# One core of a hybrid retention and attention layer: row-times-weight sums on VectorE alone, early splits on ScalarE and VectorE, and the gate's columns loaded behind the first pair's keys and values

## The chip, the core and the metric

The kernel runs on one core of one Trainium2 chip. The metric is the device time of one execution in microseconds (us), the median of the runs shown. A profiled execution has a time of its own, which is given beside its span.

## What is computed

The reference is one layer over 2048 latent tokens and 256 context tokens of width 1024, in float32. Cut to what matters here:

```python
shift, scale, gate = jnp.split(jax.nn.silu(c) @ w_ada[l] + b_ada[l], 3, axis=-1)
shift_c, scale_c, gate_c = jnp.split(jax.nn.silu(c_ctx) @ w_ada[l] + b_ada[l], 3, axis=-1)
h = rms_norm(x) * (1.0 + scale[:, None, :]) + shift[:, None, :]
hc = rms_norm(ctx) * (1.0 + scale_c) + shift_c
rq, rk, rv, rg, aq, ak, av, ag = project(h, w_in[l])
crq, crk, crv, crg, caq, cak, cav, cag = project(hc, w_in[l])
...
s_fwd = retention_final_state(crk, crv, log_gamma[0], reverse=False)
ret_x, _, _ = retention_branch(rq, rk, rv, rg, log_gamma, ret_gn_w[l], s_fwd, s_bwd)
att_x = merge_heads(windowed_gqa(aq, ak, av, cak, cav, att_sink[l])) * jax.nn.silu(ag)
mixed = jnp.concatenate([ret_x, att_x], axis=-1) @ w_out[l]
x = x + gate[:, None, :] * mixed
return rms_norm(x) * final_norm_w
```

The modulation needs three vectors of width 1024 for the latent tokens (shift, scale, gate) and two for the context (shift_c, scale_c). Each is a product of a row, silu(c) or silu(c_ctx), with a 1024 x 1024 part of w_ada.

## The kernel before, in words

**Two phases.** Up to about 600 us the kernel projects the tokens, group by group of 512 (groups 3 and 2 first, then the context, then 1 and 0), and stores queries, keys, values, gates and the states of the retention in HBM. From there on it goes block by block through retention, attention and the output projection. The change lies in the first phase.

**Precision.** A float32 product is made of three passes on TensorE: each operand is split into a high half, rounded to the engine's fast float32 form (`rounded`, line 105), and a low half, the difference. A unit of projection is 256 columns of w_in for one group: `load_w` (line 314) loads them in two parts of 512 KB each, rounds the high half and subtracts for the low half, in four pieces of 128x512 each. TensorE then makes 2 x 24 matmuls (8 blocks of the width, 3 passes each). So TensorE waits for the low halves as much as for the high ones. `split` (line 374) does the same to results that are stored as halves: the attention's queries and keys.

**The modulation sums.** `weigh` (line 209) multiplies a 128x1024 tile of the transposed w_ada with the row and sums along the row, which gives 128 numbers of a vector. With `idle` false it is one VectorE instruction with an accumulator (line 215); with `idle` true a product on GpSimd (POOL, line 212) and a copy with an accumulator on ScalarE (ACT, line 213). `ada` (line 220) calls it for the shift and the scale (j = 0 and 1) of one block of the width; for the context the scale (j = 1) is done with `idle`. `gate_columns` (line 604) calls it for eight blocks of the gate, every other one with `idle`. The context's steps (`prep_ctx`, line 246) are: load the context and make its statistics, then for each block `column(k)` (line 260): two `weigh`, the scaling on ACT (line 268), the high half on POOL (`rounded`, line 269) and the low half on VectorE (line 270).

**What sets the order.** The steps of the context and of the gate's columns stand in a list, `spare`, and `background(n)` (line 404) issues the next n of them behind a unit. The units run in the order of the list `order` (line 1040): aq1, rq0, rq1, then the first pair's keys and values rk0 and rv0 (context, group 3, group 2), then rk1 and rv1, and so on. `weights` (line 1045) loads the next units' weights ahead: two slots hold split weights (pool wp) and seven slots of 512 KB hold what has just been loaded (pool ld: parts of w_in, tiles of w_ada, rows of x). A load waits, on the one load queue of SyncE (SP), until a slot is free, and what stands behind it on that queue waits too. The framework arranges the instructions of each engine by a schedule of its own; each engine then runs its queue in that order.

**The context's keys and values** (`ctx_rk`, `ctx_rv`) are the first units that need the modulated context: tiles crk and crv on TensorE, from hc (the context's halves) and the weights w_brk and w_brv. Behind them come rk for group 3 (tile rk, 2 x 24 matmuls), the retention's context state (tile cu), and so on.

**Names in the rows.** wss is a tile of w_ada for shift and scale, wgt one for the gate; room holds the context and the two rows; w_baq, w_brq, w_brk, w_brv are split weights, wr_ in front of a name means as loaded; hi_aq and lo_aq are the halves of the attention's queries, m_aq and m_rq the products of the rotary step; xr_x are rows of x for the statistics of the next group.

Of the kernel before, what the change touches and what calls it, by code (L numbers as in the profile page):

```python
# [11 lines left out]
AF = mybir.ActivationFunctionType  # L12
# [27 lines left out]
def tile_hymba(  # L40
# [168 lines left out]
    def weigh(w, row, a, idle=False):  # L209

        if idle:
            pool.tensor_tensor(w, w, row, op=ALU.mult)
            act.activation(w, w, AF.Copy, accum_out=a)
        else:
            dve.scalar_tensor_tensor(w, w, 1.0, row, op0=ALU.mult, op1=ALU.mult, accum_out=a)
# [4 lines left out]
    def ada(pl, tag, row, kc, which, after=(None, None)):  # L220
        for j in range(2):
            w = pl.tile([P, D], F32, tag=tag, name=f"wss{which}_{kc}_{j}")
            nc.sync.dma_start(w, wss[kc][:, j, :])
            with behind(after[j]):
                weigh(w, row, acc2[:, kc, which, j : j + 1], which and j)
        dve.tensor_tensor(mod[:, kc, which], acc2[:, kc, which], nbada[:, kc:16:8], op=ALU.add)
# [24 lines left out]
    def prep_ctx():  # L251
# [9 lines left out]
        def column(k):  # L261
            if k == 0:
                r = st.spread()
                for x in xk:
                    dve.tensor_tensor(x, x, r, op=ALU.mult)
            ada(ld, "ld", row1, k, 1)
            x = xk[k]
            act.activation(x, x, AF.Identity, bias=mod[:, k, 1, 0:1], scale=mod[:, k, 1, 1:2])
            rounded(hc[0][:, k, :], x)
            dve.tensor_tensor(hc[1][:, k, :], x, hc[0][:, k, :], op=ALU.subtract)  # L270
# [43 lines left out]
    def load_w(name, uid, parts=(0, 1), w=None, lo="dve", fine=None, hi="pool"):  # L314
# [3 lines left out]
        for i in parts:  # L318
# [3 lines left out]
            for j in range(2):  # L322
# [6 lines left out]
                (pool if lo == "pool" or (lo == "mix" and j) else dve).tensor_tensor(w[:, 1, ks, :], r2, w[:, 0, ks, :], op=ALU.subtract)  # L329
# [44 lines left out]
    def split(src, name, n=GT, np_=P):  # L374
        hi = tmp(f"hi_{name}", dt=F32R)[:np_, :n]
        lo = tmp(f"lo_{name}", dt=F32R)[:np_, :n]
        rounded(hi, src)
# [27 lines left out]
    spare = []  # L405
# [200 lines left out]
    def gate_columns():  # L606
# [3 lines left out]
        def column(k):  # L610
            wg = ld.tile([P, D], F32, tag="ld", name=f"wgt{k}")
            nc.sync.dma_start(wg, wgt[k])
            weigh(wg, row2, gcol[:, k : k + 1], k % 2)
# [422 lines left out]
    spare += gate_columns()  # L1036
# [8 lines left out]
    def weights(i, ahead=1):  # L1045

        for x in order[i : i + 1 + ahead]:
            if x not in W:
                early = x in order[:3]
                W[x] = load_w(x[0], x[1] + x[0], lo="mix" if early else "dve", hi="act" if early else "pool")  # L1050
        return W[order[i]]

    def retention(i, gs, before=lambda name, g: None):

        w = weights(i), weights(i + 1, 0)
        for n, g in enumerate(gs):
            for j in range(2):
                before(order[i + j][0], g)
                unit(order[i + j][0], g, w[j])
                background()  # L1060
# [18 lines left out]
    X = []  # L1079
    retention(5, groups, ahead)  # L1080
# [325 lines left out]
```

## Time and profile before

| what | value |
| --- | --- |
| median of 3 runs | 1181.79 us (1178.88 to 1182.34) |
| profiled execution, its own time | 1177.99 us |
| its span, first to last instruction | 1175.4 us |
| TensorE (PE) busy | 1133.2 us, 96% |
| VectorE (DVE) busy | 798.2 us, 68% |
| ScalarE (ACT) busy | 465.7 us, 40% |
| GpSimd (POOL) busy | 404.5 us, 34% |

The page gives busy times over the whole span, which mix two phases with different limits. TensorE is the engine that has the least idle time, so the question in each stretch is whether it has work, at which clock, and for what it waits where it has none. The views by stretch, of waits, of the chain of work and of the engines' instructions in order of time are those that the rows below come from.

### The profile page before, as it was taken

The page shows a single profiled execution, that of the slowest core. Times are in us where ns is not written, and L with a number is a line of the kernel's source. Part 1 is how long each engine was busy: PE and PEld are TensorE (multiplying, and loading weights), DVE is VectorE, ACT ScalarE, POOL GpSimd, SP SyncE. Part 2 cuts the span into 40 slices and gives each one's busy share as a digit, 9 for nine tenths or more (in the row PEclk, how much of TensorE's full clock was granted, in tenths as well). Part 3 has the DMA queues.
Part 4 walks back from the last instruction along what each step waited for, and adds up shares of the span by engine and source line. Part 5 has one row for each costly group of instructions (what it writes and reads, how often), then busy time and mean ns, then how long its engine had stood idle before and what let it go on. Part 6 is the DMA issues. An engine that isn't in the chain of part 4 may idle for free.

```text
span 1175.4 us, 18111 instructions
## 1 busy us (share of the span) xinstructions
PE 1133.2 (96%) x6290; PEld 973.1 (83%) x6290; DVE 798.2 (68%) x1883; ACT 465.7 (40%) x1025; POOL 404.5 (34%) x517
## 2 busy tenths in 40 slices
PE   7999978999999999999999988999999999999997
PEld 3887857999988889998888877888888888888885
DVE  6974876544783645657666447777777777777774
ACT  3344423432342002331001336555555555555562
POOL 1102654100221200002224335555555555555542
PEclk9998989999999999999999999999999999999999
DMA  8948678542564542533356385444444444444310
GB/s 305 324 152 259 235 228 308 177 132 86 176 215 157 162 125 77 175 119 117 97 162 201 83 210 187 131 130 131 130 130 131 131 130 131 130 130 131 95 37 36
DMA packets 139537, 182.24 MB, mean 155 GB/s; under 512 B 11315, under 2 KB 103091, under 8 KB 139318
## 3 DMA queue, kind: packets, MB, share of 16 engines
q1 hardware_dynamic: 126630, 174.54, 47.3%
q10 hardware_dynamic: 12816, 6.56, 1.8%
q8 instruction: 49, 0.80, 0.3%
q14 instruction: 42, 0.34, 0.1%
HBM read 130.19 MB, written 50.86 MB: 154 GB/s over the span
## 4 chain that ended last, share of the span: by engine, by line
PE 69%; DVE 19%; POOL 3%; ACT 3%; DMA 3%; issue 2%; SPq 1%; DVEq 0%; POOLq 0%; ACTq 0%
PE pz L1205 10%; PE rv L354 8%; PE rk L341 7%; PE aq L341 6%; PE ag L341 6%; PE o L1168 4%; PE rg L341 4%; PE rq L341 4%; PE pt L1155 3%; DVE p L749 3%; DVE phl L1158 3%; PE S L743 3%; PE u L470 2%; PE ak L341 2%; PE S L747 2%
## 5 line engine op out<-in xcount | busy, mean ns | idle before, releaser
L1157 ACT ACTIVATE phl<-pt 128x512 fp32r<-128x512 f32 x156 | 92.7, 595 | 98.8 <-PE pt L1155 96.0
L765 POOL TENSOR_SCALAR p<-p,m 128x640 f32<-128x640 f32 (+1 forms) x128 | 104.1, 814 | 69.9 <-DVE m L764 68.5
L1158 DVE TENSOR_TENSOR phl<-pt,phl 128x512 fp32r<-128x512 f32 x156 | 106.8, 686 | 29.9 <-ACT phl L1157 29.2
L756 ACT ACTIVATE p<-p,m 128x641 f32<-128x641 f32 (+1 forms) x128 | 104.5, 816 | 47.3 <-DVE m L753 47.0
L749 DVE CUSTOM_DVE_ANT_0 p<-S,msk 128x640 f32<-128x640 f32 (+1 forms) x128 | 102.5, 801 | 23.4 <-PE S L747 22.0
L1205 PE MATMUL pz<-wg1h,ma 128*128 128x512 f32 x256 | 106.0, 419 | 0.1
L1205 PE MATMUL pz<-wg0h,mr 128*128 128x512 f32 x256 | 104.0, 409 | 0.6 <-POOL mr L1194 0.4
L1155 PE MATMUL pt<-ident,p 128*128 128x128 f32 x624 | 94.0, 273 | 0.0
L743 PE MATMUL S<-kwin,aq 128*128 128x384 f32 (+1 forms) x256 | 79.2, 332 | 4.2 <-DVE m L749 2.8
L1155 PEld LDWEIGHTS pt<-ident,p 128*128 128x128 f32 x624 | 75.8, 141 | 8.7 <-issue 0.4
L446 ACT ACTIVATE vw<-v,wdec 128x128 fp32r<-128x128 f32 x128 | 43.5, 393 | 80.1 <-DVE v L459 80.1
L747 PE MATMUL S<-kctx,aq 128*128 128x256 f32 x256 | 71.1, 280 | 0.0
L1168 PE MATMUL o<-phl,vwin 128*128 128x512 f32 x184 | 63.1, 422 | 0.8 <-DVE phl L1158 0.6
L743 PEld LDWEIGHTS S<-kwin,aq 128*128 128x128 f32 x256 | 48.0, 188 | 10.7 <-DVE m L749 3.4
L1205 PEld LDWEIGHTS pz<-wg0h,mr 128*128 128x128 f32 x256 | 48.1, 188 | 9.3 <-POOL mr L1194 0.8
L1205 PEld LDWEIGHTS pz<-wg1h,ma 128*128 128x128 f32 x256 | 48.1, 188 | 7.9 <-POOL ma L1183 0.5
L747 PEld LDWEIGHTS S<-kctx,aq 128*128 128x128 f32 x256 | 48.2, 188 | 5.3
L1168 PE MATMUL o<-phl,vctx 128*128 128x512 f32 x128 | 44.7, 414 | 6.8 <-DVE phl L1158 6.7
L1205 PE MATMUL pz<-wg0l,mr 128*128 128x512 f32 x128 | 50.5, 395 | 0.0
L1205 PE MATMUL pz<-wg1l,ma 128*128 128x512 f32 x128 | 50.3, 393 | 0.0
L448 DVE SCALAR_TENSOR_TENSOR vw<-v,wdec,vw 128x128 fp32r<-128x128 f32 x128 | 39.9, 358 | 6.2 <-ACT vw L446 6.2
L780 POOL TENSOR_TENSOR qd<-qkv,decq 128x512 f32<-128x512 f32 x30 | 42.3, 1428 | 1.1
(430 smaller groups left out, 3067.7 us busy)
## 6 DMA issues: line engine op xcount, KB each, us to landing
wss<-in_wss SPq DMA_DIRECT2D x32, 512.0 KB, 6.3
qkv<-d_qkv SPq DMA_DIRECT2D x15, 768.0 KB, 6.2
aq<-d_aq SPq DMA_DIRECT2D x64, 128.0 KB, 3.9
xb<-in_xn SPq DMA_DIRECT2D x16, 512.0 KB, 4.2
out<-xb SPq DMA_DIRECT2D x31, 256.0 KB, 2.3
st<-d_st SPq DMA_DIRECT2D x15, 512.0 KB, 3.8
x<-in_xt SPq DMA_DIRECT2D x12, 512.0 KB, 5.3
xr_x<-in_xn SPq DMA_DIRECT2D x12, 512.0 KB, 3.8
```

The lines of the kernel that those rows point to most:

```text
L341: pe.matmul(ps, w[:, a, k, c0 : c0 + P], ht[b][:, k, :], start=(k == 0 and i == 0), stop=(k == NK - 1 and i == 2),)
L354: pe.matmul(ps, ht[a][:, k, t * P : (t + 1) * P], w[:, b, k, :], start=(k == 0 and i == 0), stop=(k == NK - 1 and i == 2),)
L743: i = pe.matmul(psc[:, o:512].rearrange("p (s t) -> p s t", t=P), AQ[b][:, h, :], C2["kwin"][:, kv, hl, ksel], start=(hl == 0), stop=(hl = ...
L747: pe.matmul(psc[:, 512:768], AQ[b][:, h, :], C2["kctx"][:, kv, hl], start=(hl == 0), stop=(hl == 1))
L749: dve.tensor_tensor_reduce(out=pb[:, j, 0:n], in0=psc[:, o : o + n], in1=mk, op0=ALU.add, op1=ALU.max, scale=1.0, scalar=-3e38, accum_out= ...
L756: act.activation(pb[:, j, 0 : n + 1], pb[:, j, 0 : n + 1], AF.Exp, bias=m4[:, 1, j : j + 1], scale=0.125, accum_out=m4[:, 2, j : j + 1],)
L765: pool.tensor_scalar(pb[:, j, 0:n], pb[:, j, 0:n], m4[:, 2, j : j + 1], 0.0, op0=ALU.mult, op1=ALU.add)
L1155: pe.transpose(ppt[:, j], pb[:, j, kt * P : (kt + 1) * P], ident)
L1157: PE["phl"] = act.activation(phl[:, 0], ppt, AF.Copy)
L1158: dve.tensor_tensor(phl[:, 1], ppt, phl[:, 0], op=ALU.subtract)
L1168: pe.matmul(PO[kv], vt, PH[kt][:, hl], start=(kt == 0 and hl == 0), stop=(kt == nkt - 1 and hl == 1))
L1205: pe.matmul(PZ[n2], m[:, a, k % RH, :], WG[k // 4][c][:, k % 4, s], start=(k == 0 and i == 0), stop=(k == NK - 1 and i == 2),)
```

## The change

Four edits. `weigh` has no `idle` form any more, so that all of its calls are one VectorE instruction. The high halves in `split` and of the context are rounded on ACT and not on POOL. For the first three units' weights (aq1, rq0, rq1) the second half of the low parts, which POOL made, is made on VectorE. The gate's columns are put into `spare` only before the second pair's keys and values (rk1 and rv1), and `background` takes two steps at a time there.

```diff
-    def weigh(w, row, a, idle=False):
-
-        if idle:
-            pool.tensor_tensor(w, w, row, op=ALU.mult)
-            act.activation(w, w, AF.Copy, accum_out=a)
-        else:
-            dve.scalar_tensor_tensor(w, w, 1.0, row, op0=ALU.mult, op1=ALU.mult, accum_out=a)
+    def weigh(w, row, a):
+
+        dve.scalar_tensor_tensor(w, w, 1.0, row, op0=ALU.mult, op1=ALU.mult, accum_out=a)
...
-                weigh(w, row, acc2[:, kc, which, j : j + 1], which and j)
+                weigh(w, row, acc2[:, kc, which, j : j + 1])
...
-            rounded(hc[0][:, k, :], x)
+            rounded(hc[0][:, k, :], x, "act")
...
-                (pool if lo == "pool" or (lo == "mix" and j) else dve).tensor_tensor(w[:, 1, ks, :], r2, w[:, 0, ks, :], op=ALU.subtract)
+                dve.tensor_tensor(w[:, 1, ks, :], r2, w[:, 0, ks, :], op=ALU.subtract)
...
     def split(src, name, n=GT, np_=P):
...
-        rounded(hi, src)
+        rounded(hi, src, "act")
...
-            weigh(wg, row2, gcol[:, k : k + 1], k % 2)
+            weigh(wg, row2, gcol[:, k : k + 1])
...
     spare += prep_ctx()
-    spare += gate_columns()
     background()
...
-                W[x] = load_w(x[0], x[1] + x[0], lo="mix" if early else "dve", hi="act" if early else "pool")
+                W[x] = load_w(x[0], x[1] + x[0], hi="act" if early else "pool")
...
     def retention(i, gs, before=lambda name, g: None):
...
                 unit(order[i + j][0], g, w[j])
-                background()
+                background(2)
...
     X = []
+    spare += gate_columns()
     retention(5, groups, ahead)
```

**VectorE, around the low halves of the weights of rq1.** The first list is the kernel before (lines 329 are the low halves, 378 the low halves of the queries, 215 the sums):

```order
L370 TENSOR_TENSOR m0_aq13_1185<-m0_aq13_1185,m1_aq13_1186 128x512
L371 TENSOR_TENSOR m2_aq13_1187<-m2_aq13_1187,m3_aq13_1188 128x512
L329 TENSOR_TENSOR w_brq1_1229<-wr_brq1_0_1230,w_brq1_1229 128x512
L378 TENSOR_TENSOR lo_aq130_1196<-m0_aq13_1185,hi_aq130_1195 128x512
L378 TENSOR_TENSOR lo_aq131_1202<-m2_aq13_1187,hi_aq131_1201 128x512
L329 TENSOR_TENSOR w_brq1_1229<-wr_brq1_1_1236,w_brq1_1229 128x512
L366 TENSOR_TENSOR m0_rq02_1294<-rq020_1242,rope_r2_1292 128x512
```

The second is the changed kernel at the same place:

```order
L366 TENSOR_TENSOR m0_aq13_1182<-m0_aq13_1182,m1_aq13_1183 128x512
L367 TENSOR_TENSOR m2_aq13_1184<-m2_aq13_1184,m3_aq13_1185 128x512
L211 SCALAR_TENSOR_TENSOR wss1_4_0_1214,acc2_112<-wss1_4_0_1214,room_793 128x1024
L374 TENSOR_TENSOR lo_aq130_1193<-m0_aq13_1182,hi_aq130_1192 128x512
L266 TENSOR_TENSOR hc_794<-room_793,hc_794 128x256
L374 TENSOR_TENSOR lo_aq131_1199<-m2_aq13_1184,hi_aq131_1198 128x512
L211 SCALAR_TENSOR_TENSOR wss1_4_1_1217,acc2_112<-wss1_4_1_1217,room_793 128x1024
L325 TENSOR_TENSOR w_brq1_1224<-wr_brq1_0_1225,w_brq1_1224 128x512
L325 TENSOR_TENSOR w_brq1_1224<-wr_brq1_0_1225,w_brq1_1224 128x512
L325 TENSOR_TENSOR w_brq1_1224<-wr_brq1_1_1231,w_brq1_1224 128x512
L266 TENSOR_TENSOR hc_794<-room_793,hc_794 128x256
L325 TENSOR_TENSOR w_brq1_1224<-wr_brq1_1_1231,w_brq1_1224 128x512
```

Two more sums and two more low halves stand in VectorE's queue up to the last low half of rq1, which POOL's queue held before (there between products and roundings).

**TensorE, behind the last matmul of rq1.** Before, the row of the gate is spread (pc) and the context's units run one behind the other:

```order
L205 MATMUL pc00_1419<-room_793,ones_71 128x512
L205 MATMUL pc01_1422<-room_793,ones_71 128x512
L354 MATMUL crk00_1439<-w_brk0_1330,hc_794 128x256 x24
L354 MATMUL crk01_1465<-w_brk0_1330,hc_794 128x256 x24
L354 MATMUL crv00_1494<-w_brv0_1425,hc_794 128x256 x24
L354 MATMUL crv01_1524<-w_brv0_1425,hc_794 128x256 x24
```

In the changed kernel (left out are five rows of the next unit, rk03, 7 matmuls):

```order
L350 MATMUL crk00_1424<-w_brk0_1323,hc_794 128x256 x21
L350 MATMUL crk01_1450<-w_brk0_1323,hc_794 128x256 x21
L350 MATMUL crv00_1476<-w_brv0_1410,hc_794 128x256
L350 MATMUL crv01_1506<-w_brv0_1410,hc_794 128x256
...
L350 MATMUL crv00_1476<-w_brv0_1410,hc_794 128x256 x9
L350 MATMUL crk00_1424<-w_brk0_1323,hc_794 128x256 x2
L350 MATMUL crk01_1450<-w_brk0_1323,hc_794 128x256 x2
L350 MATMUL crk00_1424<-w_brk0_1323,hc_794 128x256
L350 MATMUL crk01_1450<-w_brk0_1323,hc_794 128x256
L350 MATMUL crv00_1476<-w_brv0_1410,hc_794 128x256 x14
L350 MATMUL crv01_1506<-w_brv0_1410,hc_794 128x256 x23
```

All of the context's keys but the last block of the width stand ahead of the values, and the two pc have gone from here; they stand between the second pair's crk and crv.

**VectorE, the gate's sums.** Before, every other one of them is on VectorE, around the first rotary step of rk0 (the last low halves of w_brv stand just ahead):

```order
L329 TENSOR_TENSOR w_brv0_1425<-wr_brv0_1_1432,w_brv0_1425 128x512 x2
L215 SCALAR_TENSOR_TENSOR wgt0_1491,gcol_115<-wgt0_1491,room_793 128x1024
L215 SCALAR_TENSOR_TENSOR wgt2_1633,gcol_115<-wgt2_1633,room_793 128x1024
L215 SCALAR_TENSOR_TENSOR wgt4_1931,gcol_115<-wgt4_1931,room_793 128x1024
L366 TENSOR_TENSOR m0_rk03_1618<-rk030_1558,rope_r3_1616 128x512
L215 SCALAR_TENSOR_TENSOR wgt6_2243,gcol_115<-wgt6_2243,room_793 128x1024
```

In the changed kernel all eight stand in one block, behind the last states of the first pair and ahead of the rotary step of rk1:

```order
L482 SCALAR_TENSOR_TENSOR rb0_8_2177<-rb0_9_2111,gC_81,u0_8_2166 128x128 x2
L211 SCALAR_TENSOR_TENSOR wgt0_2214,gcol_115<-wgt0_2214,room_793 128x1024
L211 SCALAR_TENSOR_TENSOR wgt1_2277,gcol_115<-wgt1_2277,room_793 128x1024
L211 SCALAR_TENSOR_TENSOR wgt2_2280,gcol_115<-wgt2_2280,room_793 128x1024
L211 SCALAR_TENSOR_TENSOR wgt3_2356,gcol_115<-wgt3_2356,room_793 128x1024
L211 SCALAR_TENSOR_TENSOR wgt4_2359,gcol_115<-wgt4_2359,room_793 128x1024
L211 SCALAR_TENSOR_TENSOR wgt5_2574,gcol_115<-wgt5_2574,room_793 128x1024
L211 SCALAR_TENSOR_TENSOR wgt6_2577,gcol_115<-wgt6_2577,room_793 128x1024
L211 SCALAR_TENSOR_TENSOR wgt7_2659,gcol_115<-wgt7_2659,room_793 128x1024
L611 TENSOR_TENSOR gcol_115<-gcol_115,nbada_75 128x8
L362 TENSOR_TENSOR m0_rk13_2341<-rk130_2283,rope_r3_1594 128x512
```

The loads of these tiles move with them on SP's queue, and the loads for the next group's statistics (xr_x) stand behind them there; on ACT the four squares of xr_x stand behind the second pair's crv and ahead of the first key rows (kn) of rk1.

## Rows read from the trace of the kernel before

**Rows 1.** The view by stretch, of the whole core: us from the start and length, then busy time and number of instructions of PE, PEld (weight loads), DVE, ACT and POOL, the granted TensorE clock as a share of full, the share of the DMA engines and GB/s.
```profile
114.90:186.60 71.70, 61.74 (x288) 50.13 (x287) 60.34 (x96) 27.85 (x67) 40.97 (x35) 0.95 0.75 233
163.40:167.00 3.60, 3.59 (x9) 2.85 (x10) 2.77 (x7) 1.20 (x2) 1.53 (x3) 0.51 0.91 230
201.60:330.00 128.40, 128.40 (x879) 119.79 (x878) 72.29 (x184) 43.19 (x127) 16.95 (x22) 1.00 0.48 150
330.00:600.00 270.00, 269.76 (x1448) 233.35 (x1447) 159.46 (x314) 56.48 (x153) 42.59 (x57) 1.00 0.44 133
```

**Rows 2.** What TensorE waited for from 60 to 205 us: us in total, times, longest.
```profile
PE rq L341 <- DVE w_brq L329: 6.6, 1, 6.6
PE crv L354 <- DVE w_brv L329: 2.4, 1, 2.4
PE crk L354 <- POOL hc L109: 0.6, 1, 0.6
```

**Rows 3.** The chain of work that ended last, in order of time: start, us, engine, tile, line.
```profile
147.90 6.76 DMA wss<-in_wss
...
157.03 1.27 POOL w_brq L329
...
162.75 0.60 DVE w_brq L329
...
190.79 10.90 PE rk L341 x48
201.69 1.73 PE cu L515 x8
...
244.24 2.87 PE crk L354 x24
```

**Rows 4.** VectorE's instructions from 114.9 to 186.6 us, by line and shape: count, busy us and mean ns of one, then idle time before them and what ended it.
```profile
L215 DVE SCALAR_TENSOR_TENSOR wss<-wss,room 128x1024 f32<-128x1024 f32 x8 | 9.7, 1216 | 0.0
L378 DVE TENSOR_TENSOR lo_aq<-m_aq,hi_aq 128x512 fp32r<-128x512 f32 x6 | 9.2, 1564 | 8.4 <-POOL hi_aq L109 8.4
L270 DVE TENSOR_TENSOR hc<-room,hc 128x256 fp32r<-128x256 f32 x8 | 5.2, 645 | 2.8 <-POOL hc L109 2.7
L329 DVE TENSOR_TENSOR w_brk<-wr_brk,w_brk 128x512 fp32r<-128x512 f32 x4 | 4.7, 1224 | 0.0
L329 DVE TENSOR_TENSOR w_brv<-wr_brv,w_brv 128x512 fp32r<-128x512 f32 x4 | 4.6, 1218 | 0.0
L370 DVE TENSOR_TENSOR m_aq<-m_aq,m_aq 128x512 f32<-128x512 f32 x3 | 3.5, 1168 | 0.0
L329 DVE TENSOR_TENSOR w_brq<-wr_brq,w_brq 128x512 fp32r<-128x512 f32 x4 | 2.6, 680 | 0.0
L368 DVE TENSOR_TENSOR m_aq<-aq,rope_a 128x512 f32<-128x512 f32 x3 | 2.0, 681 | 0.0
L290 DVE TENSOR_TENSOR u<-u,d 128x8 f32<-128x8 f32 x1 | 1.3, 1261 | 0.0
```

**Rows 5.** GpSimd's instructions and one group of ScalarE from 105 to 205 us, in the same form.
```profile
L212 POOL TENSOR_TENSOR wss<-wss,room 128x1024 f32<-128x1024 f32 x8 | 20.1, 2518 | 8.1 <-DMA wss<-in_wss 5.5 <-PE rr_xc L196 2.6
L109 POOL TENSOR_SCALAR w_brk<-wr_brk 128x512 fp32r<-128x512 f32 x4 | 2.6, 661 | 0.3 <-DMA wr_brk<-in_win 0.3
L109 POOL TENSOR_SCALAR w_brv<-wr_brv 128x512 fp32r<-128x512 f32 x4 | 2.5, 658 | 0.0
L111 ACT ACTIVATE w_brq<-wr_brq 128x512 fp32r<-128x512 f32 x8 | 4.4, 617 | 0.0
```

**Rows 6.** Single instructions of VectorE and GpSimd in order of time: start, us, engine, line, shapes, and in brackets the idle time before and what ended it.
```profile
127.62 2.42 POOL L212 TENSOR_TENSOR wss<-wss,room 128x1024 f32<-128x1024 f32 x1
127.69 2.90 DVE L378 TENSOR_TENSOR lo_aq<-m_aq,hi_aq 128x512 fp32r<-128x512 f32 x1 [3.19 <-POOL hi_aq L109]
149.71 0.42 DVE L270 TENSOR_TENSOR hc<-room,hc 128x256 fp32r<-128x256 f32 x1 [0.29 <-POOL hc L109]
182.00 4.64 DVE L329 TENSOR_TENSOR w_brv<-wr_brv,w_brv 128x512 fp32r<-128x512 f32 x4
186.57 1.21 DVE L215 SCALAR_TENSOR_TENSOR wgt<-wgt,room 128x1024 f32<-128x1024 f32 x1
187.71 0.08 DVE L215 DVE_READ_ACCUMULATOR wgt<-wgt,room 128x1 f32 x1
```

**Rows 7.** TensorE in order of time: the first matmul of rq0, the first behind its wait for rq1's weights, the row of the gate, the first matmul of crv and the rest behind their wait.
```profile
142.44 0.39 PE L341 MATMUL rq<-h2h,w_brq 128*128 128x512 f32 x1
...
163.41 1.22 PE L341 MATMUL rq<-h2h,w_brq 128*128 128x512 f32 x2 [6.61 <-DVE w_brq L329]
...
172.98 1.98 PE L205 MATMUL pc<-room,ones 1*128 1x512 f32 x4
...
184.89 5.89 PE L354 MATMUL crv<-w_brv,hc 128*128 128x256 f32 x47 [2.39 <-DVE w_brv L329]
```

**Rows 8.** Where the block of the gate's sums and the squares go to: VectorE's and ScalarE's first instruction behind their idle time there, TensorE's spread of the next group's statistics, and the median us to landing of a gate tile (86 to 205 us).
```profile
262.02 0.69 DVE L366 TENSOR_TENSOR m_rk<-rk,rope_r 128x512 f32<-128x512 f32 x1 [12.36 <-PE rk L341]
272.50 0.39 ACT L435 ACTIVATE kn<-pk 128x256 fp32r<-128x256 f32 x1 [14.80 <-PE pk L430]
338.77 1.05 PE L196 MATMUL rr_x<-dg_x,ones 128*128 128x128 f32 x8
wgt<-in_wgt SPq DMA_DIRECT2D x8, 512.0 KB, 6.6
```

More of the change, by code (lines that the diff above doesn't have):

```diff
@@ L312, in fine_rows, with load_w @@
         return rows
-    def load_w(name, uid, parts=(0, 1), w=None, lo="dve", fine=None, hi="pool"):
+    def load_w(name, uid, parts=(0, 1), w=None, fine=None, hi="pool"):
         ci = CHUNKS.index(name)
```

## The prediction, made before the changed kernel ran

> **What bounds the kernel now.** I read the stretches first, then TensorE's waits, then the chain of work, then VectorE's instructions by shape, and last the single instructions at the places where these meet.
>
> By stretch [rows 1], TensorE is busy for the whole of 201.6 to 330 us at the full clock (128.40 of 128.40), and for 269.76 of 270 us up to 600: what the change does there can save nothing, and costs nothing unless TensorE comes to wait. From 114.9 to 186.6 us it is busy for 61.74 of 71.70 us, while VectorE is busy for 60.34. Its waits there are few [rows 2]: 6.6 us once, for the low halves of w_brq (rq1), 2.4 us for those of w_brv, 0.6 us for the context's halves. Behind the long one the granted clock is 0.51 for 3.6 us [rows 1], the lower of the two levels. So in this stretch TensorE waits for VectorE.
>
> And VectorE waits for GpSimd. The chain [rows 3] shows how: a load of wss lands, behind the product that waited for it GpSimd makes its half of w_brq and the hi_aq that VectorE waits for, then comes VectorE's last w_brq, and then rq1. By shape [rows 4] VectorE stands 8.4 us before lo_aq and 2.7 us before hc, both for a high half from GpSimd: 11.1 us. And some of its instructions are longer than their like: lo_aq, with two operands in SBUF, takes 1564 ns where w_brq of the same shape takes 680. One pair shows why [rows 6]: GpSimd's product runs from 127.62 to 130.04 us, and the lo_aq that starts at 127.69 ends at 130.59.
>
> **What the change adds to VectorE, up to the last low half of w_brv at 186.64 us** (182.00 + 4.64, [rows 6]). Eight sums for the context's scale come from GpSimd and ScalarE. From the start of one to the end of its accumulator read are 1.22 us [rows 6], so 9.8 us. Six low halves of 128x512 (two each for aq1, rq0 and rq1) at some 0.61 us, 680 ns less the overlap with the next [rows 4]: 3.7 us. Sum **+13.5 us**. The gate's sums stand behind this point before and after.
>
> **What it takes from VectorE.** All products of GpSimd in this stretch go, the eight of 2518 ns among them [rows 5], and its hi_aq and hc too. If the high halves are ready on ScalarE in time, the 11.1 us of waiting go. ScalarE loses eight copies and gains fourteen roundings of 617 ns or less [rows 5]; it was busy 27.85 of 71.70 us [rows 1], so it has room. Then the lengthening [rows 4], each against 680 ns (hc against the 0.42 us of one that met nothing, [rows 6]): lo_aq 6 x 0.88 = 5.3, hc 8 x 0.22 = 1.8, w_brk and w_brv 8 x 0.54 = 4.3, m_aq of line 370 3 x 0.49 = 1.5, one tiny instruction of line 290 1.1. Sum 14.0 us.
>
> Not all of it goes: the eight roundings of w_brk and w_brv stay on GpSimd, 5.2 us in all [rows 5], and now meet sums with two operands in SBUF. From nothing to the whole 5.2 us can stay; I take half, 2.6 us, because the rotary products, which read PSUM, kept their 681 ns beside GpSimd's products [rows 4], and half of what now stands beside the roundings are such. The handover from ScalarE to VectorE was not seen at this place; from GpSimd it cost 0.29 us each where nothing else was late [rows 6], so between 0 and 14 x 0.29 = 4.1 us. I take 0: in the new order a sum or a rotary step stands between most roundings and their low halves.
>
> VectorE reaches the last w_brv at 13.5 - 11.1 - 14.0 + 2.6 = **9.0 us** earlier, at 177.6 us.
>
> A rule bears on the lengthening. The Trainium skill, SBUF: State Buffer, section "SBUF: two separate sides", says that VectorE and GpSimd share one port pair as an exclusive lock: whichever starts first keeps it for its whole instruction, VectorE with two SBUF inputs among the cases. The pair of instructions above agrees. By the lock alone all 5.2 us of the roundings that stay would be lost, and the sum would be 2.6 us worse than mine.
>
> **What TensorE does with it.** rq1 would start at its place, 142.44 + 10.9 = 153.3 us [rows 7, 3], and find its low halves: between the last w_brq and the last w_brv the new queue holds twelve rotary steps and eight low halves of 0.6 us, six sums of 1.22 us and some small ones, 20.6 us, so the last w_brq ends near 177.6 - 2.6 - 20.6 = 154.4 us, and TensorE takes them in order. Then come the context's units. The low half of the last block of hc stands 0.6 us ahead of the last w_brv. From it on TensorE has 2 + 14 + 23 matmuls of 256 columns left, at 2.87/24 = 0.12 us [rows 3] 4.7 us, and 41 of the 48 of rk at 10.90/48 = 0.227 us, 9.3 us; together 14.0 us, and rk ends at 177.6 - 0.6 + 14.0 = 191.0 us instead of 201.69 [rows 3]. That is 10.7 us earlier. The bound by TensorE is not reached: rq1, the context's units (4 x 2.87) and rk without a gap would end near 153.3 + 10.9 + 11.5 + 10.9 = 186.6 us.
>
> **What moves and comes back.** The row of the gate takes 1.98 us of TensorE [rows 7]. It moves to the second pair, where TensorE has no gap, so 2.0 us are only moved: they are in the old sum and must be paid again, since rk's end above is without them. Net 10.7 - 2.0 = **8.7 us**. The eight gate sums, 9.8 us, go into the 12.36 us for which VectorE stood idle before the rotary step of rk1 [rows 8]. ScalarE's four squares go into its 14.80 us [rows 8]. Eight gate loads leave the stretch in which the weights of rk0 and rv0 load, and on SP's queue stand between stores of states; the loads of xr_x and x stand behind them, for statistics that TensorE spreads at 338.77 us [rows 8]. Were the cover gone, each microsecond by which the block is late would be one for rk1's rotary step, and less for TensorE, which has five accumulators and needs two in a unit. The splits of later queries and keys (GpSimd to ScalarE) lie beside a TensorE that has no gap [rows 1]: nothing.
>
> The profiled execution takes 1177.99 us, its span 1175.4; the median of the runs shown is 1181.79. The sum is a difference, so I put it on the median: 1181.8 - 8.7 = **1173.1 us**. The measurement can tell about 0.3%, 3.5 us, from no change. With nothing kept of the lengthening the gain is 11.3 us, 1170.5; with 5.2 + 4.1 us kept it is 2.0 us, 1179.8.
>
> **Rivals.**
>
> *The loads become the bound.* GpSimd waited 5.5 us for loads of wss [rows 5]. On VectorE such a wait holds everything behind it. The second part of rq1's weights now stands on SP's queue behind a rotary table and a query store that wait for VectorE. For it: the DMA engines are at 0.75 of their time in the stretch [rows 1]. Against it: in VectorE's new queue some 18 us stand between what lets that load go and the last w_brq, and a load like it lands in 6.8 us [rows 3]. If 5.5 us are waited, the gain is 3.2 us: 1178.6 us.
>
> *Given back in the second pair.* The eighth gate tile can load only when the first sum has freed its slot; it lands 6.6 us later [rows 8], so the block takes at least 1.2 + 6.6 + 1.2 = 9.0 us of the 12.36. If stores before it hold the load back by 8 us, VectorE is some 5 us late and ScalarE's squares keep the first key rows waiting: 1178 us.
>
> *VectorE becomes the bound: slower.* Were the lengthening due to something other than GpSimd's products, for instance to loads into the same memory, the 14.0 us would stay and 13.5 be added. With 11.1 us of waits gone and 4.1 of handover come, VectorE ends 6.5 us later. The end of rk comes 1.6 us less late than that (15.0 us from the last w_brv to rk's end before, 13.4 now), and the 2.0 us come back on top: 6.9 us slower, 1188.7 us. It decides from the point at which less than about 55% of the 25.1 us goes. Against it: the pair of instructions [rows 6], and w_brq's 680 ns, which met no product.
>
> The Trainium skill speaks for this rival: Perfetto Trace Analysis, section "Optimizing Scalar/DVE Operations", advises moving work from a saturated VectorE to ScalarE or even GpSimd. The change does the reverse, and by that advice alone it would cost the 13.5 us: some 1195 us. The same passage warns that GpSimd shares a port with VectorE, and the trace agrees with the warning, in the 2.90 us of that lo_aq.
>
> **How the numbers follow.** The forecast has 0.70: order and rows agree, and the sizes are open rather than the sign. The loads have 0.13, given back 0.08, VectorE as the bound 0.09. Faster by over 0.3%: 0.66 of the forecast (its worst bound is inside 0.3%), 0.06 of the loads, 0.05 of given back, 0.77. Slower: 0.08 of the third rival. Within: 0.15. The range reaches from 1168, the best bound less the 2.9 us by which the lowest run lies under the median, to 1180, the worst bound, which takes in both middle cases.
>
> **What would show it.** Right: no wait of TensorE for w_brq, and under 2 us for w_brv and hc together; lo_aq and hc near 0.68 and 0.43 us; rk of the first pair ending near 191 us (as the trace before counts time); no new wait of TensorE from there to 600 us; the eight gate sums in one block that ends before the rotary step of rk1 is due. Wrong: lo_aq still over 1 us without GpSimd, VectorE idle before wss for a DMA, or TensorE waiting between 230 and 280 us.

## The result, and the profile after

The changed kernel takes **1167.73 us** (median of 5 runs, 1166.79 to 1168.65), the kernel before in the same comparison 1181.79 us (5 runs, 1178.88 to 1182.34): a ratio of 0.9897, interval 0.9881 to 0.9913, or 10.3 to 14.1 us. Run again beside another set of runs of the kernel before, it came to 1168.26 against 1179.30 us, 0.9909 (0.9895 to 0.9924), or 9.0 to 12.4 us. The prediction was 1173.1 us, 8.7 us faster: the direction and the place were right, the gain was undersized by some 3 us. The stated range begins at 1168 us: the first median lies 0.3 us under it, the second 0.3 us inside. The profiled execution took 1168.23 us, its span 1166.4.

The view by stretch of the changed kernel, columns as in [rows 1]; the first stretch runs from the first sum of wss to the end of the last low half of w_brv, which are now at 113.95 and 173.95 us:

```profile
113.95:173.95 60.00, 57.86 (x284) 48.61 (x283) 59.97 (x117) 21.84 (x59) 7.87 (x8) 1.00 0.87 280
187.60:316.00 128.40, 128.40 (x874) 118.75 (x873) 80.97 (x200) 45.58 (x130) 11.44 (x17) 1.00 0.53 168
316.00:586.00 270.00, 268.96 (x1444) 232.61 (x1443) 157.12 (x313) 64.75 (x167) 32.70 (x45) 1.00 0.44 135
```

The same work of VectorE took 71.70 us before [rows 1, 6], for 60.34 us of which it was busy. Now it is busy for 59.97 of 60.00 us: it does more and never stands still. GpSimd fell from 40.97 to 7.87 us. The DMA engines are busier, 0.87 instead of 0.75.

VectorE by shape in that stretch, as [rows 4]:

```profile
L211 DVE SCALAR_TENSOR_TENSOR wss<-wss,room 128x1024 f32<-128x1024 f32 x16 | 19.7, 1239 | 0.0
L374 DVE TENSOR_TENSOR lo_aq<-m_aq,hi_aq 128x512 fp32r<-128x512 f32 x6 | 4.1, 681 | 0.0
L266 DVE TENSOR_TENSOR hc<-room,hc 128x256 fp32r<-128x256 f32 x8 | 3.7, 462 | 0.0
L325 DVE TENSOR_TENSOR w_brv<-wr_brv,w_brv 128x512 fp32r<-128x512 f32 x4 | 2.6, 686 | 0.0
L325 DVE TENSOR_TENSOR w_brk<-wr_brk,w_brk 128x512 fp32r<-128x512 f32 x4 | 2.6, 681 | 0.0
L366 DVE TENSOR_TENSOR m_aq<-m_aq,m_aq 128x512 f32<-128x512 f32 x3 | 2.0, 678 | 0.0
L286 DVE TENSOR_TENSOR u<-u,d 128x8 f32<-128x8 f32 x1 | 0.2, 160 | 0.0
```

Read it against [rows 4] shape by shape: lo_aq 1564 to 681 ns, w_brk 1224 to 681, w_brv 1218 to 686, the m_aq with two operands in SBUF 1168 to 678, the tiny u 1261 to 160. The column of waiting is 0.0 everywhere: the 8.4 and 2.8 us have gone.

TensorE's waits from 60 to 205 us, as [rows 2]:

```profile
PE crv L350 <- DVE w_brv L325: 1.5, 1, 1.5
PE ss_xc L168 <- DVE sqc L165: 1.1, 1, 1.1
PE aq L337 <- ACT g L587: 0.7, 1, 0.7
PE crk L350 <- DVE w_brk L325: 0.6, 1, 0.6
```

The wait of 6.6 us for w_brq has no successor. The chain of work (start, us, engine, tile), as [rows 3]:

```profile
178.36 9.32 PE rk L337 x41
187.68 1.73 PE cu L511 x8
...
236.66 1.91 PE pc L205 x4
...
244.52 10.91 PE rk L337 x48
```

Here the gain can be followed. The first rk ends at 187.68 instead of 201.69 us [rows 3], 14.0 us earlier. The row of the gate (pc) is paid for at 236.66 us, and the first rk of the second pair starts at 244.52 instead of 256.52 us, 12.0 us earlier.

### The profile page after: what moved, and what is told of

The parts are those of the page before. It is cut to its first block, busy times and chain, and to the rows that moved or that the text cites. A ratio compares the mean times of both kernels' runs of the same rounds, so it can differ in the third digit from the quotient of the medians.

```text
span 1166.4 us, 18074 instructions
## 1 busy us (share of the span) xinstructions
PE 1131.5 (97%) x6290; PEld 972.9 (83%) x6290; DVE 795.5 (68%) x1913; ACT 471.1 (40%) x1035; POOL 344.2 (30%) x465
## 4 chain that ended last, share of the span: by engine, by line
PE 65%; DVE 17%; issue 5%; POOL 3%; ACT 3%; DMA 2%; SPq 0%; DVEq 0%; POOLq 0%; ACTq 0%
PE pz L1201 10%; PE rv L350 8%; PE rk L337 7%; PE ag L337 6%; PE o L1164 4%; PE rg L337 4%; PE aq L337 4%; PE rq L337 4%; PE pt L1151 3%; DVE p L745 3%; DVE phl L1154 3%; PE S L739 2%; PE u L466 2%; PE ak L337 2%; PE S L743 2%
```

## The experiments

Twelve more runs were made, one of them the changed kernel again. For each, two numbers are set beside each other here: the start of the first cu on TensorE (by the list of its instructions in order of time, that is, the end of the first rk) and the median time. The kernel before had medians of 1181.79, 1179.83, 1180.02 and 1179.30 us in the four comparisons.

| kernel | first cu, us | median, us |
| --- | --- | --- |
| before | 201.53 | 1179.30 to 1181.79 |
| sums and low halves only (edits 1, 3) | 196.62 | 1175.42 |
| high halves only (edit 2) | 199.93 | 1178.48 |
| all but the columns (edits 1 to 3) | 190.91 | 1170.20 |
| columns only (edit 4) | 200.49 | 1179.14 |
| changed | 187.51 | 1167.73 |
| changed, again | 187.22 | 1168.26 |
| + 32 products on GpSimd | 196.51 | 1177.07 |
| + 64 roundings on GpSimd | 195.88 | 1176.46 |
| + 16 sums on VectorE | 204.77 | 1188.45 |
| + first pair's roundings on ScalarE | 185.86 | 1168.92 |
| rows spread by loads | 190.30 | 1172.25 |
| columns early, their row by a load | 188.24 | 1169.19 |
| rows by loads, all roundings on ScalarE | 188.31 | 1168.34 |

**Edits 1 and 3 alone.** The kernel before with

```diff
-                weigh(w, row, acc2[:, kc, which, j : j + 1], which and j)
+                weigh(w, row, acc2[:, kc, which, j : j + 1], False)
-            weigh(wg, row2, gcol[:, k : k + 1], k % 2)
+            weigh(wg, row2, gcol[:, k : k + 1], False)
-                W[x] = load_w(..., lo="mix" if early else "dve", ...)
+                W[x] = load_w(..., lo="dve", ...)
```

Expected: 

> The kernel before with the sums of the context and of the gate on VectorE alone and the low halves of aq1, rq0 and rq1 on VectorE (edits 1 and 3); the high halves of the context and of the queries stay on GpSimd, the gate's columns stay early. Theory (GpSimd's products hold VectorE): 13.5 us are added, most of the 14.0 us of lengthening goes, and the 11.1 us of waiting for high halves shrink to some 4 us, since no product stands ahead of them in GpSimd's queue: VectorE 5 us earlier, the time 1172 to 1178 us; lo_aq below 1 us. Rival (VectorE is the bound and the lengthening has another cause): lo_aq stays near 1.5 us and the time rises by 5 us or more, to 1186 us or more.

Measured: 1175.42 us (ratio 0.9956, 0.9944 to 0.9969), inside the theory's range. VectorE by shape from 114.9 to 187 us:

```profile
L378 DVE TENSOR_TENSOR lo_aq<-m_aq,hi_aq 128x512 fp32r<-128x512 f32 x6 | 5.7, 984 | 0.2 <-POOL hi_aq L109 0.2
L270 DVE TENSOR_TENSOR hc<-room,hc 128x256 fp32r<-128x256 f32 x8 | 3.8, 478 | 1.5 <-POOL hc L109 1.5
```

More work on VectorE made the kernel faster. The waits for GpSimd fell to 1.7 us by themselves, with the high halves still made there: what had made them late was the work ahead of them in GpSimd's queue, the products above all. lo_aq stays at 984 ns, beside GpSimd's roundings.

**Edit 2 alone.** The kernel before with

```diff
-            rounded(hc[0][:, k, :], x)
+            rounded(hc[0][:, k, :], x, "act")
-        rounded(hi, src)
+        rounded(hi, src, "act")
```

Expected: 

> The kernel before with only the high halves of the context and of the queries moved from GpSimd to ScalarE (edit 2). Theory: the 11.1 us of waiting before lo_aq and hc go, but GpSimd's products still run beside VectorE, so lo_aq, hc, w_brk and w_brv stay lengthened (lo_aq over 1.3 us); rq1 still waits for the low halves that GpSimd makes behind its products. Between 0 and 8 us faster: 1172 to 1181 us. Rival (the waits alone made the gain, the products do no harm): the gain of the whole change, 1168 to 1170 us, with lo_aq at 0.7 us.

Measured: 1178.48 us (0.9988, 0.9977 to 0.9998). VectorE by shape, then TensorE's waits:

```profile
L378 DVE TENSOR_TENSOR lo_aq<-m_aq,hi_aq 128x512 fp32r<-128x512 f32 x6 | 9.9, 1659 | 6.7 <-ACT hi_aq L111 6.7
...
PE pc L205 <- DMA room<-in_crow: 5.9, 1, 5.9
```

The products still lengthen lo_aq. And, against what I expected, the wait before it did not go: 6.7 us, now for ScalarE, whose queue also holds the copies that sum GpSimd's products. TensorE's 6.6 us turned into 5.9 us before pc, whose row stands on SP's queue behind stores of the queries, which wait for ScalarE's high halves and VectorE's low halves. The edits need each other: 4.4 and 1.4 us apart, 9.6 together (next run).

**Edits 1 to 3, the columns early.** The changed kernel with edit 4 taken back:

```diff
     spare += prep_ctx()
+    spare += gate_columns()
...
-                background(2)
+                background()
...
-    spare += gate_columns()
     retention(5, groups, ahead)
```

Expected: 

> The changed kernel with the gate's columns put back to where they were (edit 4 undone, edits 1 to 3 kept). Theory: the gate's sums stand behind the last low half of w_brv either way; only the 2.0 us of TensorE for the row of the gate come back into a stretch in which TensorE waits for some 2 us, so 0 to 2 us slower than the changed kernel: 1168 to 1170.5 us. Rival (the loads bound the stretch, and moving the gate's eight loads made the gain): 3 us or more slower than the changed kernel, 1171 to 1178 us, with VectorE idle for a DMA before wss or w_brk.

Measured: 1170.20 us (0.9912, 0.9895 to 0.9928). TensorE waits for nothing between 105 us and the first cu, which all the same starts 3.4 us later than in the changed kernel. Rows of TensorE in order of time, and one of the stretches (the granted clock is third from the end), show most of it:

```profile
164.36 0.39 PE L337 MATMUL rq<-h2h,w_brq 128*128 128x512 f32 x1
164.68 1.98 PE L205 MATMUL pc<-room,ones 1*128 1x512 f32 x4
...
166.60:170.60 4.00, 4.00 (x22) 4.00 (x22) 4.00 (x7) 0.60 (x1) 2.83 (x4) 0.57 0.51 207
```

The pc itself takes 2.0 us, and for 4 us behind it the clock is 0.57 of full, which costs 1.7 us more. TensorE was granted the lower level without having waited. Another 2.4 us were lost earlier: the last matmul of rq1 starts at 164.36 us, in the changed kernel at 162.01. Its TensorE starts 0.8 us later at 103 us and has a longer stretch at the lower clock up to 115 us (0.57 and 0.75 of full in two halves of 5 us, against 0.73 and 0.92). This is far ahead of the place of edit 4, and the changed kernel's second trace has that matmul at 163.32 us. Against the 6.1 us stand 2.1 us of waiting that the changed kernel has here and this run has not; that leaves 4.0 us, of which 3.4 came. The time lies in the theory's range, and its interval overlaps that of the changed kernel: what edit 4 is worth, 1.9 to 2.5 us by the medians, is not clear of the noise.

**Edit 4 alone**, the kernel before with those three lines moved:

Expected: 

> The kernel before with only the gate's columns moved behind the first pair (edit 4; their sums still half on GpSimd). Theory: the stretch up to the last low half of w_brv keeps its waits and its lengthening; no more than the 2.0 us of the row of the gate change their place: 1179 to 1183 us, not to be told from no change. Rival (the loads): 3 to 9 us faster, 1172 to 1178 us.

Measured: 1179.14 us (0.9996, 0.9983 to 1.0009), no change, as the theory had it. TensorE still waits 5.9 us for w_brq.

**Is it GpSimd, or the loads?** The changed kernel, its queues on VectorE, TensorE and ScalarE unchanged, with products that nobody reads:

```diff
             dve.tensor_tensor(hc[1][:, k, :], x, hc[0][:, k, :], op=ALU.subtract)
+            for q in range(4):
+                pool.tensor_tensor(row2[:, q * CTX : (q + 1) * CTX], x, x, op=ALU.mult)
```

Expected: 

> The changed kernel, with 32 products of 128x256 on GpSimd in the context's stretch (four for each block of the width, both operands in SBUF, into an area that nobody reads); the queues of VectorE, TensorE and ScalarE are word for word those of the changed kernel, and no load is added. By the products of the kernel before they are some 0.6 us each, 19.3 us. Theory (GpSimd's products lengthen VectorE's instructions with two operands in SBUF): of 27 us of GpSimd's products the lengthening was 14.0 us before, so about half of the 19.3 us comes on VectorE, the end of rk 7 to 12 us later, the time 1175 to 1181 us, with wss, lo_aq and the low halves above their usual length. Rival (the loads lengthen them): no change, 1166.5 to 1169 us.

Measured: 1177.07 us (0.9975 of before, 0.9962 to 0.9988), some 9 us of the gain lost; the first cu 9.0 us later. VectorE by shape from 113.5 to 187 us:

```profile
L211 DVE SCALAR_TENSOR_TENSOR wss<-wss,room 128x1024 f32<-128x1024 f32 x16 | 20.9, 1316 | 0.0
L266 DVE TENSOR_TENSOR hc<-room,hc 128x256 fp32r<-128x256 f32 x8 | 6.3, 784 | 0.0
L376 DVE TENSOR_TENSOR lo_aq<-m_aq,hi_aq 128x512 fp32r<-128x512 f32 x6 | 5.8, 958 | 0.0
L369 DVE TENSOR_TENSOR m_rq<-m_rq,m_rq 128x512 f32<-128x512 f32 x2 | 2.2, 1094 | 0.0
L367 DVE TENSOR_TENSOR m_rq<-rq,rope_r 128x512 f32<-128x512 f32 x2 | 1.4, 676 | 0.0
```

The last two rows are the cleanest sign in this study: the same shape, beside the same products, takes 1094 ns where both operands are in SBUF and 676 ns where one is in PSUM. Single instructions in order of time show the size of one meeting, first GpSimd's, then VectorE's:

```profile
136.03 3.62 POOL L268 TENSOR_TENSOR room<-room 128x256 f32<-128x256 f32 x4 [8.28 <-ACT room L264]
```

```profile
136.32 1.09 DVE L376 TENSOR_TENSOR lo_aq<-m_aq,hi_aq 128x512 fp32r<-128x512 f32 x1
137.33 0.83 DVE L266 TENSOR_TENSOR hc<-room,hc 128x256 fp32r<-128x256 f32 x1
138.08 1.10 DVE L376 TENSOR_TENSOR lo_aq<-m_aq,hi_aq 128x512 fp32r<-128x512 f32 x1
139.10 1.63 DVE L211 SCALAR_TENSOR_TENSOR wss<-wss,room 128x1024 f32<-128x1024 f32 x1
```

Each is longer than its like by about 0.41 us, whatever its own length (0.68, 0.42, 0.68, 1.21 us): it is held once, and GpSimd's products are held in turn (3.62 us for four, where the shortest single one took 0.61). A delay that does not grow with the instruction's own length points at a lock that changes hands between instructions, not at shared bandwidth. The Trainium skill states such a lock (SBUF — State Buffer, "SBUF: two separate sides"); these rows agree with it.

**VectorE's slack.** The changed kernel with

```diff
                 weigh(w, row, acc2[:, kc, which, j : j + 1])
+                if which:
+                    weigh(w, row, dum[:, kc, j : j + 1])
```

Expected: 

> The changed kernel with each of the context's sixteen sums made a second time on VectorE, in a column that nobody reads: 16 x 1.22 = 19.5 us more on VectorE, no load and no work of GpSimd added. Theory (VectorE's queue sets the end of the context's keys and values, with no slack): 16 to 21 us slower than the changed kernel, 1184 to 1189 us, and TensorE waits that long for VectorE. Rival (TensorE or the loads set it, VectorE has slack): 0 to 8 us slower, 1168 to 1176 us.

Measured: 1188.45 us (1.0080 of before, 1.0064 to 1.0097), 20 us slower than the changed kernel for 19.5 us of work. TensorE's waits from 60 to 215 us:

```profile
PE rq L340 <- DVE w_brq L328: 10.7, 1, 10.7
PE crv L353 <- POOL w_brv L109: 6.8, 1, 6.8
```

The second wait is put down to GpSimd's rounding of w_brv. It is VectorE's too: the loads of w_brv are issued from 174.0 us on, when VectorE's last sums end, and GpSimd stands 8.2 us idle for them. The first cu starts 17.3 us later; where the other 3 us arise was not read. So VectorE has next to no slack there: work that is added to it and that nothing offsets goes onto the time, which is the rival that the prediction feared.

**The roundings that stay**, on ScalarE:

```diff
-                early = x in order[:3]
+                early = x in order[:5]
```

Expected: 

> The changed kernel with the high halves of the first pair's weights (w_brk and w_brv, eight roundings) on ScalarE too; the queues of VectorE and TensorE are word for word the same. Theory (the 1.5 us of lengthening that stay, at the sums and low halves between 157 and 162.5 us, come from GpSimd's roundings): VectorE 1.5 us earlier, TensorE's 2.1 us of waiting there shrink to about 0.6 us, the time 1 to 1.5 us lower, 1166 to 1167 us. Rival (they come from the loads, or ScalarE is late with the roundings): 1167.5 to 1170 us, and the sum beside them stays at 1.6 us.

Measured: 1168.92 us (0.9908, 0.9890 to 0.9925), not to be told from the changed kernel. In place it did what the theory says: the sum at 157 us is back at 1.22 us, the first cu comes 1.65 us earlier (1.36 against the changed kernel's second trace), and TensorE waits for nothing from 105 us to it. The time, all the same, lies in the rival's range. The stretch behind pc (at 235.01 us here) shows one thing that took it back:

```profile
236.00:242.00 6.00, 6.00 (x33) 5.24 (x32) 4.07 (x7) 2.24 (x5) 0.00 (x0) 0.72 0.57 187
```

6 us at 0.72 of the clock cost 1.7 us; behind the same pc the changed kernel kept the full clock (1.00 from 236.00 to 245.00 us).

**Products or roundings?** As the products, but

```diff
+            for q in range(8):
+                pool.tensor_scalar(row2[...], x, 1.0, 0.0, op0=ALU.mult, op1=ALU.add)
```

Expected: 

> As the run with the products, but with 64 roundings of 128x256 (one operand in SBUF) instead of the 32 products: at half of the 0.66 us of w_brk's 128x512 they are 21 us, the same load on GpSimd in time. If GpSimd's time is what counts, whatever its operands: as much as the products, 1175 to 1181 us. If only its instructions with two operands in SBUF hold VectorE: no change, 1166.5 to 1169 us. The half that the prediction took for such roundings would be 5 us: 1171 to 1175 us.

Measured: 1176.46 us (0.9973, 0.9963 to 0.9983), as much as the products. VectorE and GpSimd by shape:

```profile
L376 DVE TENSOR_TENSOR lo_aq<-m_aq,hi_aq 128x512 fp32r<-128x512 f32 x6 | 4.9, 812 | 0.0
...
L268 POOL TENSOR_SCALAR room<-room 128x256 f32<-128x256 f32 x64 | 40.6, 663 | 30.7 <-ACT room L264 30.7
```

Two instructions of VectorE in order of time, at the same place as with the products:

```profile
136.13 0.87 DVE L376 TENSOR_TENSOR lo_aq<-m_aq,hi_aq 128x512 fp32r<-128x512 f32 x1
...
138.26 1.41 DVE L211 SCALAR_TENSOR_TENSOR wss<-wss,room 128x1024 f32<-128x1024 f32 x1
```

Each meeting costs less, 0.2 us and not 0.41, but there are twice as many. The roundings took 40.6 us instead of the 21 that I had put, so part of the 8 us is w_brk's and w_brv's roundings, which stand behind them (TensorE waited 3.2 us for those of w_brv). A rounding on GpSimd, with one operand, holds VectorE too: "only products do" has fallen.

**The changed kernel again**, without an edit:

Expected: 

> The changed kernel once more, beside the following runs on the same chip. Nothing is changed. It settles what the size of the gain is with more runs of both kernels: from the runs of before in the two studies so far (medians 1179.8 and 1180.0 us) 12 us, 1167 to 1169 us; from the first comparison 14 us.

Measured: 1168.26 us against 1179.30. Taken with the first comparison, 10 to 12 us lie in both intervals.

**Rows spread by loads.** The changed kernel with, for both rows,

```diff
-            silu_row(row1, 1)
+            silu_wide(row1, 1)
+    def silu_wide(t, i):
+        nc.sync.dma_start(t, crow[i].partition_broadcast(P))
+        act.activation(t, t, AF.Silu)
```

Expected: 

> The changed kernel with the rows silu(c_ctx) and silu(c) of the context's stretch and of the gate spread over the partitions by a load of 512 KB each and one ScalarE instruction, instead of by TensorE (the pc matmuls, 2 x 1.98 us at full clock). Theory (TensorE's time counts wherever it has no gap, and the stretches at the lower clock that follow a pc cost some 1.8 us each): 2 to 6 us faster than the changed kernel, 1162 to 1166 us, with the granted clock at 1.0 around 105 us and 238 us. Rival (the load of the first row is late, and with it the first sum of VectorE): VectorE's queue starts later by 2 to 4 us and nothing is gained, 1167 to 1171 us.

Measured: 1172.25 us (0.9934, 0.9914 to 0.9954): the rival, and 1 us above its range. Without the pc the clock does stay up around 107 us, by stretch:

```profile
105.00:110.00 5.00, 5.00 (x24) 4.14 (x23) 0.00 (x0) 3.44 (x5) 0.00 (x0) 1.00 1.03 405
```

(0.73 in the changed kernel.) But the first sum starts at 115.66 instead of 113.95 us, TensorE waits for the low halves, and behind the first of these waits the clock falls after all (0.72 from 115 to 120 us):

```profile
PE aq L341 <- DVE w_baq L329: 2.6, 1, 2.6
PE crk L354 <- DVE w_brk L329: 1.9, 1, 1.9
```

What TensorE gained, VectorE's queue lost.

**Columns early, their row by a load** (the third run with `silu_wide(row2, 0)`):

Expected: 

> The changed kernel with the gate's columns early (as in the run with edit 4 undone), but the gate's row spread by a load, so that no pc stands between rq1 and the context's keys. It tells apart what made edit 4 worth 2.5 us. Theory (the 2.0 us of pc and the 1.8 us of lower clock behind it): the end of the first rk comes 3 us or more earlier than with edit 4 undone, at 187 to 188 us, and the time is that of the changed kernel or lower by the 2 us of pc that it never pays: 1165 to 1168 us. Rival (the gate's loads in the stretch): rk ends at 190 us or later, 1169 to 1171 us.

Measured: 1169.19 us (0.9908, 0.9893 to 0.9923). The first cu starts at 188.24 us: 2.7 of the 3.4 us come back with the gate's loads still in the stretch. The granted clock is 1.00 from 160 to 188 us. So most of it was the pc and its clock and not the loads; 0.5 of the 2.7 us were there before the end of rq1. The time, however, lies in the rival's range and not in the theory's: the 2 us that pc no longer costs do not show in it. TensorE waits 1.1 us for VectorE and ScalarE between 204 and 222 us, where the changed kernel has no wait; the rest was not read.

**Rows by loads, no roundings on GpSimd** (`hi="act"` for all weights of the first phase):

Expected: 

> As the run with both rows by loads, and with the high halves of all weights of the first phase on ScalarE, so that GpSimd rounds none of them. Theory: the first pair's 1.5 us of lengthening go, and w_bag's low halves and the lo_ak beside them near 330 us (1.08 us instead of 0.68) too, so that TensorE's wait of 1.0 us for the modulation there shrinks: 1 to 3 us lower than with the rows alone, 1160 to 1165 us. Rival (what is gained in one place is taken back as a lower clock or as a late ScalarE): within 1 us of it or slower.

Measured: 1168.34 us (0.9909, 0.9893 to 0.9926). The theory's range is missed. The median is 3.9 us below that of the run with the rows alone (3 us was the most expected; the two intervals overlap), and no better than the changed kernel. Near 330 us the theory holds, TensorE's wait is gone. But it now waits 3.6 us for the low halves of w_brq near 153 us (1.1 with the rows alone), and the clock behind that wait is 0.82 from 155 to 160 us: gained in one place and taken back in another, as the rival has it. No version that ran beats the changed kernel.

## Why the prediction was right, and where it was too small

**The mechanism** was right, and is shown from both sides: taking GpSimd's products out of the stretch made VectorE's instructions short and its waits vanish, and putting useless ones back brought the long instructions and 9 us back.

**Added work, 13.5 us.** A shade high. A sum takes 1.14 us from its start to the next instruction's, since the read of the accumulator lies beside that: 0.6 us less over eight sums.

**Waits, 11.1 us.** All gone (60.34 of 71.70 us busy before, 59.97 of 60.00 after), and no handover came in their place, as taken.

**Lengthening, 14.0 us of which 2.6 kept.** 1.55 us were kept. They all stand beside w_brk's roundings:

```profile
157.08 5.41 POOL L109 TENSOR_SCALAR w_brk<-wr_brk 128x512 fp32r<-128x512 f32 x4 [52.55 <-PE rq L337]
165.02 2.46 POOL L109 TENSOR_SCALAR w_brv<-wr_brv 128x512 fp32r<-128x512 f32 x4 [2.53 <-DMA wr_brv<-in_win]
```

```profile
158.02 1.62 DVE L211 SCALAR_TENSOR_TENSOR wss<-wss,room 128x1024 f32<-128x1024 f32 x1
...
159.57 0.55 DVE L222 TENSOR_TENSOR mod<-acc,nbada 128x2 f32<-128x2 f32 x1
...
161.25 0.77 DVE L266 TENSOR_TENSOR hc<-room,hc 128x256 fp32r<-128x256 f32 x1
161.94 0.56 DVE L222 TENSOR_TENSOR mod<-acc,nbada 128x2 f32<-128x2 f32 x1
...
173.27 0.68 DVE L325 TENSOR_TENSOR w_brv<-wr_brv,w_brv 128x512 fp32r<-128x512 f32 x1
```

0.41, 0.40, 0.34 and 0.40 us too long. GpSimd lost more: its four roundings took 5.41 us where w_brv's four, which met rotary steps, took 2.46. To take half was right in kind (what reads PSUM is not held), but which half had to be read from the order of the instructions: w_brv's met almost nothing else. All 5.2 us, the prediction's figure by the lock alone, would have needed every rounding to meet an instruction with two operands in SBUF. The sum of this stretch came out at 11.7 us instead of 9.0: 0.6 from the sums, 1.05 from the kept lengthening, 0.3 of waiting beyond the 11.1, and 0.8 us that I can't assign.

**The start.** The prediction let VectorE start at the same time; the first sum starts 1.0 us earlier (113.95 instead of 114.94 us). It stands behind two tiny instructions that wait for small loads, and in the other kernels that spread this row with pc it starts anywhere from 113.2 to 114.8 us. So this 1.0 us is not shown to come from the change; it may be luck. With it the last low half of w_brv ends 12.7 us earlier, at 173.95 us; forecast 177.6.

**TensorE.** 14.0 us from the last low half of hc to the end of rk were forecast. It was 14.3 (from 173.35 to 187.68 us). So **the step that was mis-sized is VectorE's sum**, 9.0 us forecast and 12.7 measured, 11.7 of it in the stretch and 1.0 at its start; with it rk's end came 14.0 us earlier and not 10.7.

**pc, 2.0 us to pay back.** Exactly so: 14.0 us at the first cu, 12.0 at the second pair's rk. In the run with edit 4 undone, pc at its old place brought a stretch at the lower clock with it; in the kernel before it did not (1.00 from 172.9 to 180 us). Whether edit 4 is worth more than nothing, which is what the prediction gave it, is not shown.

**The gate's sums at no cost.** Right. The block, first, last and what follows (VectorE in order of time):

```profile
239.51 1.23 DVE L211 SCALAR_TENSOR_TENSOR wgt<-wgt,room 128x1024 f32<-128x1024 f32 x1 [3.96 <-ACT room L206]
...
247.54 1.22 DVE L211 SCALAR_TENSOR_TENSOR wgt<-wgt,room 128x1024 f32<-128x1024 f32 x1
...
250.03 0.69 DVE L362 TENSOR_TENSOR m_rk<-rk,rope_r 128x512 f32<-128x512 f32 x1 [1.06 <-PE rk L337]
```

Eight sums in a row, none waiting for its load, and 1.06 us left before the rotary step is due. The rival "given back in the second pair" did not come.

**No new wait up to 600 us.** Nearly: one of 1.0 us, where it was 0.2:

```profile
PE pvx L536 <- DVE x L227: 1.0, 1, 1.0
```

It stands in the runs of edits 1 and 3 (1.1 us) and of edit 2 (1.1), and not in that of edit 4 (0.2).

**The rivals.** VectorE never waited for a load of wss, with the DMA engines at 0.87. VectorE did become what TensorE waits for, as the slower rival says, but without the 14.0 us that made it slower. The advice that spoke for that rival (the Trainium skill, Perfetto Trace Analysis, "Optimizing Scalar/DVE Operations") would have kept the products on GpSimd; its warning about the shared port weighed more here.

**The end.** From 12.0 us at 245 us, 11.2 are left at 600 us, in keeping with the 10 to 12 us that both comparisons allow. The 14.1 us between the first comparison's medians owe some 2 us to its kernel before, whose median is 1.8 to 2.5 us above those of the other three. The profiled pair shows 9.8: behind 680 us both traces of the changed kernel have at least one more stretch at the lower clock than the one of the kernel before. Such stretches differ from run to run, and most that were read here cost some 1.7 us; what sets them off was not settled.

## What to carry to other kernels

An instruction of VectorE that is longer than its like of the same shape can point at GpSimd: find what runs there at that moment before calling VectorE full. Moving work from GpSimd onto a VectorE that seems to be the bound can then make VectorE's queue shorter; count the lengthening and the waits that go against the work that comes, and read from the order which instructions will stand beside what stays. A gain that is shown at the place of the change can be eaten later by a few microseconds at the lower clock, so follow it along the chain to the end.

## What the runs showed of the hardware

- GpSimd's one-operand roundings hold VectorE as its products do, and both lose: a 128x256 rounding took 398 ns at the least and 663 on average beside VectorE's sums, a 128x256 product 607 and 882.
- The delay goes with GpSimd's instruction, and is some 0.2 us shorter than that: 2.22 us beside a 128x1024 product of 2.42 [rows 6], 0.41 beside a 128x256 product (0.61 at the least) and beside a 128x512 rounding (0.66 [rows 5]), 0.2 beside a 128x256 rounding (0.40 at the least).
- Even a 128x2 VectorE instruction with two operands in SBUF was held, 0.55 us instead of 0.15 (mod, above). In the kernel before, one of 128x8 with a single operand was too, which ended as GpSimd's product did (first GpSimd's, then VectorE's); in the changed kernel it took 0.17 us:

```profile
111.77 2.40 POOL L212 TENSOR_TENSOR wss<-wss,room 128x1024 f32<-128x1024 f32 x1
```

```profile
112.29 1.90 DVE L284 TENSOR_SCALAR d<-u 128x8 f32<-128x8 f32 x1 [2.60 <-DMA d_g<-g]
```

- Broadcasting a row by matmuls with one row of weights (pc, 2 us) was followed by the lower clock in some kernels (0.57 for 4 us with the columns early, 0.72 for 6 us with the roundings on ScalarE) and not in others (1.00 in the changed kernel's second one), and without it the stretch around 107 us kept the full clock.
